# A two-layer HGRN2 and FNet kernel: gates of heads 4 to 15 as two-by-two block products of seven parts

## The chip, the cores and the metric

The kernel runs on one core of a Trainium2 chip. The metric is the time of one execution in device microseconds (us). The engines are named as in the profile: PE (TensorE, matmuls), PEld (its weight loads), DVE (VectorE), ACT (ScalarE), POOL (GpSimd) and SP (SyncE, which issues the DMAs).

## What is computed

There are 512 latent tokens, 256 context tokens, a width of 1024 and two layers. Layer 0 is a bidirectional gated recurrence (HGRN2) of 16 heads of 128, layer 1 a Fourier mixing. The core of the reference for layer 0:

```python
def hgrn_project(h, w_in, lb):
    p = (h @ w_in).reshape(B, N, 5, 16, 128)          # 5 streams, 16 heads
    q = silu(p[0])
    f = lbh + (1.0 - lbh) * sigmoid(p[1:3])           # forget gates, both directions
    return q, 1.0 - f, log(f), p[3], p[4]             # q, k, g, v, z

def hgrn_mixer(h_ctx, h_lat, ...):
    qc, kc, gc, vc, zc = hgrn_project(h_ctx, w_in, lb)
    ql, kl, gl, vl, zl = hgrn_project(h_lat, w_in, lb)
    o_cf, s_cf = chunk_scan(qc, kc[0], vc, gc[0], s0) # context, forward
    o_cb, s_cb = chunk_scan(flip(qc), flip(kc[1]), flip(vc), flip(gc[1]), s0)
    o_lf, _ = chunk_scan(ql, kl[0], vl, gl[0], s_cf)  # latents start from its state
    o_lb, _ = chunk_scan(flip(ql), flip(kl[1]), flip(vl), flip(gl[1]), s_cb)
    y = rms_norm(o_lf + flip(o_lb), norm_g) * silu(zl)
    return heads_joined(y) @ w_out                    # w_out: 2048 x 1024
```

Here h is the RMS-normalized, modulated input of a layer; its output, times a gate row, is added to the residual. Layer 1 is a product, a two-dimensional Fourier transform over tokens and channel groups, and an output product.

## The kernel before

Every matrix product is made in three parts (`mm3`, L94): each fp32 operand is split into a rounded high half and a rest, and hi·hi, hi·lo and lo·hi are added up in PSUM. The tokens after modulation stand transposed in SBUF as `hlh` and `hll` (latents, 8 tiles of 128 x 512) and `hc` (context, 128 x 256), high and low. `Weights` (L59) loads raw weights `wr` of 128 x 1024 into three buffers by SP, and splits them into `wh` (ACT, L56) and `wl` (DVE, L57), one tile ahead of its use.

`projections` takes the heads in pairs: `proj` (L449) of an even head, the pair's values (`proj_v`, tiles `vps`), `proj` of the odd head. A head's projection is two gates, each a latent product `pf` (24 matmuls of 512 columns) and a context product `pfc` (24 of 256), then q and z (`pq`, 24 of 512 each). Head 0 is made in the start.

`scan` (L494) is one head's recurrence, a generator that is stepped once for each projection step (`advance`, L717), so that a head's scan runs beside the next projection: an even head's levels beside the values, an odd head's beside the next head's gates. A scan has seven levels. In a level PE makes `gp` (L578) of `kk` and `z`, DVE multiplies `z` by the decay (L586, two instructions) and takes `gp` into `am` under a mask (L605), and ACT copies the new `kk` (L545), from which the next `gp` comes. Then follow `ktp`, `sp`, `op`, the norm `rstd_o` on POOL (L179, L180), the transposes `otp` and the output `y`.

`ada_rest` (L377) adds up the other modulation rows, `acc` (L401, DVE), from 32 pieces `ar` that are fetched into two buffers. The 13 outputs of the first heads are taken into the output product `o0a` (`out0_early`, `out0_late`) from pairs of `y` in SBUF.

From the end of the start on, a list scheduler sets each engine's order, by dependencies and a priority from the order of the program. An engine carries out its instructions in that order, and waits at one whose inputs are not there.

Of the kernel before, what the change touches and what calls it, by code (L numbers as in the profile page):

```python
# [32 lines left out]
def hgrn_fourier_kernel(ctx: ExitStack, tc: tile.TileContext, a):  # L33
# [25 lines left out]
    class Weights:  # L59
# [5 lines left out]
        def loaded(self, n):  # L65
            while len(self.raw) <= min(n, len(self.specs) - 1):
                src, shape, _ = self.specs[len(self.raw)]
                j = len(self.raw)
                raw = pw.tile(shape, F32, tag="wr", name=f"wr{j}")
                nc.sync.dma_start(out=raw, in_=src)  # L70
                self.raw.append(raw)

        def halves(self, n):
            while len(self.parts) <= min(n, len(self.specs) - 1):
                j = len(self.parts)
                self.loaded(j)
# [48 lines left out]
    masks = pc.tile([P, 7, P], U8, name="masks")  # L125
# [4 lines left out]
    ones_r = pc.tile([P, P], F32R, name="ones_r")  # L130
# [53 lines left out]
    hlh = ph.tile([P, KT, T], F32R, tag="hlh", name="hlh")  # L184
    hll = ph.tile([P, KT, T], F32R, tag="hll", name="hll")
    hc4 = [[ph.tile([P, KT // 2, TC], F32R, tag=f"hc{b}{j}", name=f"hc{b}{j}") for j in range(2)] for b in range(2)]
    hlat = ([hlh[:, k, :] for k in range(KT)], [hll[:, k, :] for k in range(KT)])
    hctx = tuple([hc4[b][k // 4][:, k % 4, :] for k in range(KT)] for b in range(2))
# [45 lines left out]
    def modulate(d, e):  # L234
# [14 lines left out]
    at = {}  # L249

# [44 lines left out]
    with tc.manual_schedule(engines={mybir.EngineType.PE, mybir.EngineType.Activation, mybir.EngineType.DVE}):  # L295
        first = {}

        def product(j, k):
# [3 lines left out]
            mm3(first[st], W.parts[j][0][:, k, :], W.parts[j][1][:, k, :], hlh[:, k, :], hll[:, k, :], k == 0, k == KT - 1)  # L302
# [53 lines left out]
    mraw = p0.tile([P, 7, P], F32, tag="junk", name="mraw")  # L356
    nc.sync.dma_start(out=mraw, in_=a["masks"])
    g.tensor_copy(masks, mraw)
    for t, src in ((own_m, ident), (near_m, mraw[:, 0, :])):
        msum = p0.tile([P, 32], F32, tag="msum", name=f"msum{t.name}", bufs=2) if t is near_m else own_m  # L360
        g.tensor_tensor(out=msum, in0=src[:, 0:32], in1=src[:, 32:64], op=ALU.add)
# [13 lines left out]
    sp = st_hgrn.enter_context(tc.tile_pool(name="sp", bufs=1))  # L375

    def ada_rest():  # L377
# [11 lines left out]
        for j in (0, 1, 2, 3):  # L389
# [4 lines left out]
            for k in range(KT):  # L394
                fetch()
                yield
                raw = raws[j * KT + k]
                if k == 0 and j in (1, 2):
                    v.tensor_scalar(out=acc, in0=raw, scalar1=scol[:, 0, k:k + 1], scalar2=None, op0=ALU.mult)
                else:  # L400
                    v.scalar_tensor_tensor(out=acc, in0=raw, scalar=scol[:, 0, k:k + 1], in1=acc,  # L401
                                           op0=ALU.mult, op1=ALU.add)
            yield
            if j in (0, 3):
                for h in range(2):
                    q = psM(f"gtp{j}_{h}")
                    pe.matmul(q, ones[:, :P], acc[:, h * 512:(h + 1) * 512], start=True, stop=True)
                    s.activation(gates[0 if j == 0 else 1][:, h * 512:(h + 1) * 512], q, AF.Copy)
# [40 lines left out]
    def proj(i):  # L449
        fl = sp.tile([P, 2, T], F32, tag="fl", name=f"fl{i}", bufs=2)  # L450
        z4 = sp.tile([P, 4, T], F32, tag="z4", name=f"z4_{i}", bufs=2)
        fc = sp.tile([P, 2, TC], F32, tag="fc", name=f"fc{i}", bufs=2)

        def gate(src, dst, col):
            s.activation(dst, src, AF.Sigmoid)
            s.activation(dst, dst, AF.Identity, scale=omlb[:, col:col + 1], bias=lbc[:, col:col + 1])

        def ctx_gate(st, wh, wl):
            pcx = (psG if i == 0 else psP)(f"pfc{i}_{st}")
            for k in range(KT):  # L460
# [10 lines left out]
        def silu(pl, dst):  # L471
            s.activation(dst, pl, AF.Sigmoid)
            v.tensor_tensor(out=dst, in0=pl, in1=dst, op=ALU.mult)
            if dst is q:
                v.tensor_tensor(out=z4[:, 0:2, :], in0=fl, in1=q.unsqueeze(1).broadcast_to([P, 2, T]), op=ALU.mult)

        if i == 0:
            for st in (1, 2):
                lat_gate(st, first[st])
            silu(first[0], q)  # L480
            for st in (1, 2):
                wh, wl = W.get(at["w", i, st])
                ctx_gate(st, wh, wl)
            silu(first[3], zs)
            W.get(at["w", i, 3])
            yield scan(i, fl, z4, fc, q, zs)
            return
        for st in (1, 2):
            wh, wl = W.get(at["w", i, st])
            pl = psP(f"pf{i}_{st}")  # L490
            yield from lat_proj(pl, wh, wl, hlh, hll)
            lat_gate(st, pl)
            yield None
            ctx_gate(st, wh, wl)  # L494
            yield None
        for st, dst in ((0, q), (3, zs)):
            wh, wl = W.get(at["w", i, st])
            pl = psP(f"pq{i}_{st}")
            yield from lat_proj(pl, wh, wl, hlh, hll)
# [3 lines left out]
            else:  # L503
                yield scan(i, fl, z4, fc, q, zs)

    def scan(i, fl, z4, fc, q, zs):
        vc = (i % 2) * P
        st = sp.tile([P, 2, NT, P], F32, tag="st", name=f"st{i}")
        kc = fc
        kct = sp.tile([P, 4, P], F32, tag="os", name=f"kct{i}")  # L510

        def ctx_decay():
            v.tensor_tensor_scan(out=rr[:, 0, TC - 2::-1], data0=fc[:, 0, TC - 1:0:-1], data1=ones[:, :TC - 1],
                                 initial=1.0, op0=ALU.mult, op1=ALU.mult)
            v.tensor_tensor_scan(out=rr[:, 1, 1:TC], data0=fc[:, 1, 0:TC - 1], data1=ones[:, :TC - 1],
                                 initial=1.0, op0=ALU.mult, op1=ALU.mult)
            s.activation(kc, fc, AF.Identity, scale=-1.0, bias=1.0)
            v.tensor_tensor(out=kc, in0=kc, in1=rr, op=ALU.mult)

        def ctx_turn():  # L520
            tp = psM(f"ctp{i}")
            for e in range(2):
                for n in range(NTC):
                    b = e * 2 + n
                    pe.transpose(tp[:, b * P:(b + 1) * P], kc[:, e, n * P:(n + 1) * P], ident)
# [43 lines left out]
        tt = fl  # L569
        h = 1  # L570
        for lev in range(7):
            nb = T // h
            gp = None
# [6 lines left out]
            for e in range(2):  # L580
                za = view(z4, e * (T + h), [[2 * T, 2], [2 * h, T // (2 * h)], [1, h]])
                if e == 0:
                    ta = view(tt, 1, [[nb, 2], [2, nb // 2], [0, h]])
                else:
                    ta = view(tt, nb, [[-nb, 2], [2, nb // 2], [0, h]])
                v.tensor_tensor(out=za, in0=za, in1=ta, op=ALU.mult)  # L586
# [20 lines left out]
            v.tensor_tensor(out=tn, in0=view(tt, 0, [[nb, 2], [2, nb // 2]]), in1=view(tt, 1, [[nb, 2], [2, nb // 2]]),  # L607
# [423 lines left out]
```

## Time and profile before

| what | value |
|---|---|
| median of 3 runs | 1209.05 us (1208.63 to 1210.82) |
| the profiled execution | 1208.84 us, span 1207.0 us, mean granted PE clock 0.995 |
| PE busy | 98% of the span |
| DVE busy | 63% |
| ACT busy | 47% |
| POOL busy | 4% |
| read from HBM, written | 115.20 MB, 2.10 MB |

An engine's share is its busy time by the span. Matmuls overlap, so the time from one start to the next tells more than one's duration. Views used below: busy time by stretches of the span, groups of instructions by line and shape (busy us, mean ns | idle time ahead of them and what ended it), single instructions in order of time (start, us), and the waits of an engine.

### The profile page before, as it was taken

The numbers are of one execution on the slowest core, as the hardware profiler recorded it, in microseconds if no ns is written. First come the engines' busy times: TensorE is split into PE (matmuls) and PEld (weight loads), VectorE is DVE, ScalarE is ACT, GpSimd is POOL, SyncE is SP. The second block draws the span as 40 slices with busy tenths as digits, with TensorE's granted clock in tenths as the row PEclk, the third lists the DMA queues.
The fourth block names the chain that finished last, engine by engine and source line by source line (L and its number), as shares of the span: only waits on it lengthen the run. The fifth ranks groups of instructions, "written<-read, shape, count | busy, mean of one in ns | idle before, by whom it ended". The sixth has DMA issues, their size and how long they took to land.

```text
span 1207.0 us, 18983 instructions
## 1 busy us (share of the span) xinstructions
PE 1186.8 (98%) x7677; PEld 1050.8 (87%) x7677; DVE 763.6 (63%) x1250; ACT 562.6 (47%) x1130; POOL 42.8 (4%) x76
## 2 busy tenths in 40 slices
PE   8999999999999999999999999999999999999997
PEld 5699899899889989989988988998888998988885
DVE  5596654665765675686457547458576856668554
ACT  4455544554454453445445455355556533333322
POOL 2100000000000000000000000000000000000000
PEclk9999999999999999999999999999999999999999
DMA  9434211122511521242121112113555314333221
GB/s 358 183 123 141 71 53 53 53 71 70 168 59 31 174 78 53 71 140 71 36 70 53 35 54 70 37 53 107 163 179 182 111 43 134 108 108 120 88 87 70
DMA packets 33673, 118.52 MB, mean 98 GB/s; under 512 B 3879, under 2 KB 4144, under 8 KB 33586
## 3 DMA queue, kind: packets, MB, share of 16 engines
q1 hardware_dynamic: 33586, 117.32, 29.6%
q8 instruction: 60, 0.98, 0.3%
q14 instruction: 27, 0.22, 0.1%
HBM read 115.20 MB, written 2.10 MB: 97 GB/s over the span
## 4 chain that ended last, share of the span: by engine, by line
PE 90%; DVE 4%; DMA 2%; ACT 2%; issue 1%; POOL 1%; SPq 0%; DVEq 0%; POOLq 0%; ACTq 0%
PE gp L578 7%; PE pf L95 4%; PE pq L95 4%; PE pq L97 4%; PE pq L96 4%; PE pf L97 4%; PE pf L96 4%; PE vps L95 4%; PE vps L96 4%; PE vps L97 4%; PE pfc L95 2%; PE pfc L96 2%; PE pfc L97 2%; PE o0a L97 2%; PE o0a L95 2%; PE o0a L96 2%
## 5 line engine op out<-in xcount | busy, mean ns | idle before, releaser
L56 ACT ACTIVATE wh<-wr 128x1024 fp32r<-128x1024 f32 x140 | 148.0, 1058 | 229.9 <-PE pq L96 89.3
L57 DVE TENSOR_TENSOR wl<-wr,wh 128x1024 fp32r<-128x1024 f32 x140 | 170.7, 1220 | 100.4 <-ACT wh L56 100.2
L586 DVE TENSOR_TENSOR z<-z,tt 128x512 f32<-128x512 f32 x192 | 124.0, 687 | 122.3 <-PE gp L578 110.9
L578 PE MATMUL gp<-z,kk 128*128 128x128 f32 x768 | 103.5, 277 | 0.7 <-ACT kk L545 0.6
L578 PEld LDWEIGHTS gp<-z,kk 128*128 128x128 f32 x768 | 97.6, 191 | 6.7 <-ACT kk L545 3.3
L95 PE MATMUL pf<-hlh,wh 128*128 128x512 f32 x240 | 99.2, 413 | 0.0
L95 PE MATMUL pq<-hlh,wh 128*128 128x512 f32 x240 | 97.1, 405 | 0.0
L545 ACT ACTIVATE kk<-z 128x512 f32<-128x512 f32 x96 | 61.8, 644 | 71.5 <-DVE z L586 71.3
L97 PE MATMUL pf<-hlh,wl 128*128 128x512 f32 x240 | 94.5, 394 | 0.0
L97 PE MATMUL pq<-hlh,wl 128*128 128x512 f32 x240 | 93.9, 391 | 0.0
L96 PE MATMUL pf<-hll,wh 128*128 128x512 f32 x240 | 93.7, 391 | 0.0
L96 PE MATMUL pq<-hll,wh 128*128 128x512 f32 x240 | 93.5, 390 | 0.0
L95 PE MATMUL pfc<-hc,wh 128*128 128x256 f32 x256 | 74.8, 292 | 0.0
L95 PE MATMUL vps<-wh,hlh 128*128 128x256 f32 x256 | 74.2, 291 | 0.0
L97 PE MATMUL vps<-wh,hll 128*128 128x256 f32 x256 | 72.6, 283 | 0.0
L96 PE MATMUL vps<-wl,hlh 128*128 128x256 f32 x256 | 72.5, 283 | 0.0
L96 PE MATMUL pfc<-hc,wh 128*128 128x256 f32 x256 | 72.4, 283 | 0.0
L97 PE MATMUL pfc<-hc,wl 128*128 128x256 f32 x256 | 72.4, 283 | 0.0
L97 PEld LDWEIGHTS pf<-hlh,wl 128*128 128x128 f32 x240 | 45.0, 188 | 10.4 <-issue 0.2
L97 PEld LDWEIGHTS pq<-hlh,wl 128*128 128x128 f32 x240 | 45.1, 188 | 10.0
L95 PEld LDWEIGHTS pf<-hlh,wh 128*128 128x128 f32 x240 | 45.2, 188 | 9.5 <-issue 1.9
L96 PEld LDWEIGHTS pf<-hll,wh 128*128 128x128 f32 x240 | 45.3, 189 | 8.2 <-issue 0.2
(268 smaller groups left out, 2994.0 us busy)
## 6 DMA issues: line engine op xcount, KB each, us to landing
wr<-hg_w SPq DMA_DIRECT2D x64, 512.0 KB, 3.5
ar<-ada_r SPq DMA_DIRECT2D x32, 512.0 KB, 3.8
wr<-ft_w SPq DMA_DIRECT2D x32, 512.0 KB, 4.0
wr<-hg_wout SPq DMA_DIRECT2D x29, 512.0 KB, 3.5
wa<-ada_a SPq DMA_DIRECT2D x16, 512.0 KB, 10.5
wr<-hg_v SPq DMA_DIRECT2D x16, 512.0 KB, 3.4
wr<-ft_wout SPq DMA_DIRECT2D x16, 512.0 KB, 3.5
xs<-x SPq DMA_DIRECT2D x4, 512.0 KB, 3.7
```

What stands on the lines that cost most here:

```text
L56: s.activation(hi, src, AF.Copy)
L57: v.tensor_tensor(out=lo, in0=src, in1=hi.bitcast(F32), op=ALU.subtract)
L95: pe.matmul(out, lh, rh, start=first, stop=False)
L96: pe.matmul(out, lh, rl, start=False, stop=False)
L97: pe.matmul(out, ll, rh, start=False, stop=last)
L545: s.activation(view(kk, 0, [[2 * h, T // (2 * h)], [h, 2], [1, h]]), view(z4, 2 * T, [[2 * h, T // (2 * h)], [T + h, 2], [1, h]]), AF.Copy)
L578: pe.matmul(gp[:, n * P:(n + 1) * P], kk[:, n * P:(n + 1) * P], view(z4, n * P, dims), start=True, stop=True)
L586: v.tensor_tensor(out=za, in0=za, in1=ta, op=ALU.mult)
```

## The change

For heads 4 to 15 the two gate weights (as 2 x 2 blocks of four k-tiles each) times the tokens (2 x 2 blocks: k-tiles 0 to 3 and 4 to 7, by even and odd tiles of 128 tokens, latents and context joined to 768 columns) are made with seven products, `px`, in place of eight. Each has 12 matmuls of 384 columns (three runs of 128), so a head has 84 of them for 48 of 512 and 48 of 256.

- `blocks` makes the products and puts them together: two copies on ACT, five adds on DVE and two on POOL, each of 128 x 384; the sums stand in `ff` (768 columns a direction), and sigmoid and lower bound run over all 768.
- `fold_piece` makes the mixed weight pieces in place in the raw tiles (four DVE instructions of 128 x 512 a head). There are seven pieces of 128 x 512 to split for two weights of 128 x 1024, taken up to four ahead.
- `mixes`, stepped every second projection step, makes four mixed token blocks once, in four rounds over the first heads: POOL adds high and low (2 x 128 x 768, into `whole`, in the buffers that `ar` and `acc` use later) and mixes (4 x 128 x 384); then four splits on ACT and DVE.
- `ar` has one buffer, its fetch follows the accumulation before, `ada_rest` begins after step 40, and two of its first products move to ACT.
- `y` of heads 0 to 12 is written to DRAM (`yd`) and fetched back in pieces of 128 x 256; the gate rows go through DRAM (`grow`).
- `ks` and `pn` take `kk`'s buffers; `am`'s copies of level 0 come ahead of the first `kk`; the masks are loaded and cast earlier, five of seven planes.

```diff
+                if j in pieces:
+                    both = pw.tile([P, 2, KT // 2, P], F32R, tag="wh" if pieces[j] % 2 else "wl", name=f"wp{j}")
+                    hi, lo = both[:, 0], both[:, 1]
...
-            self.halves(n + 1)
+            if n in pieces and pieces[n] < 5:
+                self.halves(min(n + 4, n + 6 - pieces[n]))
+            else:
+                self.halves(n + 2 if n + 2 in pieces else n + 1)
...
+    def fold_piece(w, j):
+        p = pieces[j]
+        w.loaded(j - p + 1)
+        f1, f2 = w.raw[j - p], w.raw[j - p + 1]
+        a11, a12, a21, a22 = f1[:, :4], f1[:, 4:], f2[:, :4], f2[:, 4:]
+        if p == 2:
+            v.tensor_tensor(out=a21, in0=a21, in1=a22, op=ALU.add)
+            v.tensor_tensor(out=a11, in0=a21, in1=a11, op=ALU.subtract)
+        elif p == 4:
+            v.tensor_tensor(out=a21, in0=a22, in1=a11, op=ALU.subtract)
+        elif p == 5:
+            v.tensor_tensor(out=a12, in0=a12, in1=a11, op=ALU.subtract)
+        return (a11, a12, a11, a21, a21, a12, a22)[p]
+
+    def head_specs(i):
+        if i < PLAIN:
+            for st in (1, 2):
+                spec(("w", i, st), a["hg_w"][i, st], [P, KT, P])
+        else:
+            for p in range(7):
+                pieces[len(specs)] = p
+                spec(("f", i, p), a["hg_w"][i, 1 + p] if p < 2 else None, [P, KT, P], fold_piece)
...
+    grow = [pd.tile([1, D], F32, name=f"grow{j}") for j in range(2)]
+    gates = [None, None]
+    yd = [pd.tile([P, T], F32, name=f"yd{i}") for i in range(13)]
...
+    def mixes():
+        for t in range(4):
+            mix[t] = [ph.tile([P, KT // 2, N // 2], F32R, tag=f"t{2 * t + b}", name=f"mix{t}_{b}") for b in range(2)]
+        for k in range(KT // 2):
+            whole = []
+            for e, tag in enumerate(("ar", "acc")):
+                t = sp.tile([P, D], F32, tag=tag, name=f"whole{k}_{e}")
+                kk = 4 * e + k
+                g.tensor_tensor(out=t[:, :N], in0=hlh[:, kk, :].bitcast(F32), in1=hll[:, kk, :].bitcast(F32), op=ALU.add)
+                w = t[:, :N].rearrange("p (n e c) -> p e n c", e=2, c=P)
+                whole += [w[:, 0], w[:, 1]]
+            b11, b12, b21, b22 = whole
+            yield
+            g.tensor_tensor(out=b22, in0=b22, in1=b12, op=ALU.subtract)
+            g.tensor_tensor(out=b12, in0=b12, in1=b11, op=ALU.subtract)
+            g.tensor_tensor(out=b11, in0=b22, in1=b11, op=ALU.add)
+            g.tensor_tensor(out=b21, in0=b21, in1=b11, op=ALU.subtract)
+            yield
+            for t, src in ((2, b22), (0, b12), (1, b11), (3, b21)):
+                split(*(mix[t][b][:, k, :].rearrange("p (n c) -> p n c", c=P) for b in range(2)), src)
+                if t in (0, 3):
+                    yield
...
-                raw = sp.tile([P, D], F32, tag="ar", name=f"ar{j}_{k}", bufs=2)
+                raw = sp.tile([P, D], F32, tag="ar", name=f"ar{j}_{k}")
...
-                fetch()
...
-                    v.tensor_scalar(out=acc, in0=raw, scalar1=scol[:, 0, k:k + 1], scalar2=None, op0=ALU.mult)
+                    s.activation(acc, raw, AF.Copy, scale=scol[:, 0, k:k + 1])
                 else:
                     v.scalar_tensor_tensor(out=acc, in0=raw, scalar=scol[:, 0, k:k + 1], in1=acc,
                                            op0=ALU.mult, op1=ALU.add)
+                fetch()
...
+    def blocks(i, ff, gate):
+        base = at["f", i, 0]
+        nh = N // 2
+
+        def out(st, half):
+            return ff[:, 2 - st].rearrange("p (n e c) -> p e n c", e=2, c=P)[:, half]
+
+        def tri(t):
+            return t[:, :nh].rearrange("p (n c) -> p n c", c=P)
+
+        def prod(p, rhs):
+            acc = psP(f"px{i}_{p}")
+            hi, lo = W.get(base + p)
+            for k in range(KT // 2):
+                mm3(tri(acc), hi[:, k, :], lo[:, k, :], rhs(0, k), rhs(1, k), k == 0, k == KT // 2 - 1)
+            return acc
+
+        def block(kh, half):
+            return lambda b, k: tiled[b][:, kh * 4 + k, half]
+
+        def mixed(t):
+            return lambda b, k: mix[t][b][:, k, :].rearrange("p (n c) -> p n c", c=P)
+
+        def kept(acc, name):
+            c = sp.tile([P, nh], F32, tag="cc", name=f"{name}{i}", bufs=2)
+            s.activation(c, acc[:, :nh], AF.Copy)
+            return c
+
+        def add(eng, dst, x, y):
+            eng.tensor_tensor(out=dst, in0=x, in1=y, op=ALU.add)
+
+        u = kept(prod(0, block(0, 0)), "u")
+        yield None
+        add(v, out(1, 0), tri(prod(1, block(1, 0))), tri(u))
+        yield None
+        add(v, u, prod(2, mixed(1))[:, :nh], u)
+        yield None
+        c5 = kept(prod(3, mixed(0)), "c5")
+        add(g, out(1, 1), tri(u), tri(c5))
+        yield None
+        add(v, u, prod(4, mixed(2))[:, :nh], u)
+        add(g, out(2, 1), tri(u), tri(c5))
+        yield None
+        add(v, out(1, 1), tri(prod(5, block(1, 1))), out(1, 1))
+        s.activation(ff[:, 1, :], ff[:, 1, :], AF.Sigmoid)
+        gate(1)
+        yield None
+        add(v, out(2, 0), tri(prod(6, mixed(3))), tri(u))
+        s.activation(ff[:, 0, :], ff[:, 0, :], AF.Sigmoid)
+        gate(2)
+        yield None
...
-        if i % 2 == 0:
-            ypair[0] = py.tile([P, 2, T], F32, tag=f"yp{i // 2}", name=f"y{i}")
-        y = ypair[0][:, i % 2, :]
+        y = py.tile([P, T], F32, tag="y" if i < LAST else f"y{i}", name=f"y{i}")
+        if i < LAST:
+            nc.sync.dma_start(out=yd[i], in_=y)
...
+    def y_fetch(k, r, ahead):
+        n = back[r].index((k, r))
+        for kk, _ in back[r][:n + 1 + ahead]:
+            if (kk, r) not in got:
+                t = got[kk, r] = (fp if r else sp).tile([P, 256], F32, tag="yr" if r else "cc", name=f"yr{r}_{kk}",
+                                                        bufs=3 if r else 2)
+                nc.sync.dma_start(out=t, in_=yd[kk][:, r * 256:(r + 1) * 256])
+        return got[k, r]
...
-        if step > 30 and step % 3 == 0:
+        if step % 2 == 0:
+            next(mix_work, None)
+        if step > 40 and step % 3 == 0:
             next(side_work, None)
```

Where instructions move. First DVE during head 3's levels, which run beside head 4's gates (z_3 and am are head 3's, px and u head 4's; a name's last number is an instance). Before:

```order
L605 COPY_PREDICATED am_2211<-masks,gp_1_2254 128x512 [waits Activation_49]
L586 TENSOR_TENSOR z_3_1891<-z_3_1891,tt_1_2264 128x2x64x4 [waits PE_49,Activation_49]
L586 TENSOR_TENSOR z_3_1891<-z_3_1891,tt_1_2264 128x2x64x4 [waits DVE_49]
L605 COPY_PREDICATED am_2211<-masks,gp_2_2300 128x512 [waits DVE_49]
L57 TENSOR_TENSOR wl_2422<-wr_2194,wh_2421 128x1024 [waits DMAHW4_49,Activation_49]
L513 SCALAR_TENSOR_TENSOR rr<-fc_2187,ones 128x255 [waits Activation_49]
L586 TENSOR_TENSOR z_3_1891<-z_3_1891,tt_2_2310 128x2x32x8 [waits PE_49,Activation_49]
```

Now:

```order
L725 COPY_PREDICATED am_2270<-masks,gp_1_2316 128x512 [waits Activation_49]
L603 TENSOR_TENSOR u_2266<-px_2_2335,u_2266 128x384 [waits DVE_49,PE_49]
L59 TENSOR_TENSOR wl_2466<-wr_2399,wh_2465 128x1024 [waits DMAHW4_49,Activation_49]
L706 TENSOR_TENSOR z_3_1949<-z_3_1949,tt_1_2326 128x2x64x4 [waits PE_49,Activation_49]
L706 TENSOR_TENSOR z_3_1949<-z_3_1949,tt_1_2326 128x2x64x4 [waits DVE_49]
L725 COPY_PREDICATED am_2270<-masks,gp_2_2352 128x512 [waits DVE_49]
L706 TENSOR_TENSOR z_3_1949<-z_3_1949,tt_2_2362 128x2x32x8 [waits PE_49,Activation_49]
L706 TENSOR_TENSOR z_3_1949<-z_3_1949,tt_2_2362 128x2x32x8 [waits DVE_49]
L725 COPY_PREDICATED am_2270<-masks,gp_3_2380 128x512 [waits DVE_49]
L603 TENSOR_TENSOR u_2266<-px_4_2398,u_2266 128x384 [waits PE_49,Pool_49]
L59 TENSOR_TENSOR wl_2506<-wr_2431,wh_2505 128x1024 [waits DMAHW6_49,Activation_49]
L706 TENSOR_TENSOR z_3_1949<-z_3_1949,tt_3_2390 128x2x16x16 [waits PE_49,Activation_49]
```

The adds of `px_2` and `px_4` and a whole split each have come between one level's z and the next; the second of the adds also waits for POOL.

Then DVE during head 5's levels, with `acc` of `ada_rest` (now; before, these levels hold no `acc`):

```order
L725 COPY_PREDICATED am_3243<-masks,gp_1_3292 128x512 [waits Activation_49]
L466 SCALAR_TENSOR_TENSOR acc_3179<-ar_2_3372,scol,acc_3179 128x1024 [waits DMAHW5_49,DVE_49]
L603 TENSOR_TENSOR u_3239<-px_2_3308,u_3239 128x384 [waits DVE_49,PE_49]
L706 TENSOR_TENSOR z_5_2911<-z_5_2911,tt_1_3302 128x2x64x4 [waits PE_49,Activation_49]
L706 TENSOR_TENSOR z_5_2911<-z_5_2911,tt_1_3302 128x2x64x4 [waits DVE_49]
L725 COPY_PREDICATED am_3243<-masks,gp_2_3325 128x512 [waits DVE_49]
L59 TENSOR_TENSOR wl_3439<-wr_3375,wh_3438 128x1024 [waits DMAHW0_49]
L466 SCALAR_TENSOR_TENSOR acc_3179<-ar_3_3479,scol,acc_3179 128x1024 [waits DMAHW7_49,DVE_49]
```

Each `acc` waits for a fetch that starts after the `acc` before it, and the next level's z stands behind it.

Last, ACT during head 0's levels 3 and 4 (`kk_16` makes gp_4, `kk_32` gp_5). Before:

```order
L545 ACTIVATE kk_16_900<-z_0_643 128x512 [waits DVE_49,Activation_49]
L56 ACTIVATE wh_993<-wr_727 128x1024 [waits DMAHW1_49,PE_49]
L545 ACTIVATE kk_32_943<-z_0_643 128x512 [waits DVE_49,Activation_49]
L440 ACTIVATE vt_722<-vps_4_911 128x512 [waits PE_49]
L56 ACTIVATE wh_1098<-wr_733 128x1024 [waits DMAHW5_49]
```

Now:

```order
L664 ACTIVATE kk_16_912<-z_0_642 128x512 [waits DVE_49,Activation_49]
L58 ACTIVATE mix_0_790<-whole_1_1118 128x384 [waits Pool_49]
L58 ACTIVATE mix_0_786<-whole_0_1116 128x384 [waits Pool_49]
L58 ACTIVATE mix_0_788<-whole_0_1116 128x384 [waits Pool_49]
L58 ACTIVATE mix_0_792<-whole_1_1118 128x384 [waits Pool_49]
L664 ACTIVATE kk_32_955<-z_0_642 128x512 [waits DVE_49,PE_49,Activation_49]
```

Four copies of the mixing's second round, each of which waits for POOL, have come ahead of `kk_32`. On POOL, head 0's `rstd_o` now stands behind all 24 adds of the mixing; before, nothing stood ahead of it but the start's work.

More of the change, by code (lines that the diff above doesn't have):

```diff
@@ L181, in rstd_of @@
         return r
[L184 to L188, printed above, removed]
+    N = T + TC
+    hlh = ph.tile([P, KT, N], F32R, name="hlh")
+    hll = ph.tile([P, KT, N], F32R, name="hll")
+    tiled = [t.rearrange("p k (n e c) -> p k e n c", e=2, c=P) for t in (hlh, hll)]
+    mix = [None] * 4
+    hlat = ([hlh[:, k, :T] for k in range(KT)], [hll[:, k, :T] for k in range(KT)])
+    hctx = ([hlh[:, k, T:] for k in range(KT)], [hll[:, k, T:] for k in range(KT)])
     acol = pc.tile([P, KT, 2], F32, name="acol")
@@ L315, in hgrn_fourier_kernel @@
             nc.sync.dma_start(out=xs[:, NT + n, :], in_=a["ctx"][n * P:(n + 1) * P, :])
+        mraw = p0.tile([P, 5, P], F32, name="mraw")
+        nc.sync.dma_start(out=mraw, in_=a["masks"][:, :5, :])
         keep_warm(24, "warm1")
@@ L348, in hgrn_fourier_kernel @@
             product(j, KT - 1)
+        g.tensor_copy(masks, mraw[:, 1:])
+        for t, src in ((own_m, ident), (near_m, mraw[:, 0, :])):
+            msum = p0.tile([P, 32], F32, tag="msum", name=f"msum{t.name}", bufs=2) if t is near_m else own_m
+            g.tensor_tensor(out=msum, in0=src[:, 0:32], in1=src[:, 32:64], op=ALU.add)
+            for j in (64, 96):
+                g.tensor_tensor(out=msum, in0=msum, in1=src[:, j:j + 32], op=ALU.add)
+            if t is near_m:
+                g.tensor_copy(near_m, msum)
         for d in range(2):
@@ L407, in ada_rest @@
                     pe.matmul(q, ones[:, :P], acc[:, h * 512:(h + 1) * 512], start=True, stop=True)
-                    s.activation(gates[0 if j == 0 else 1][:, h * 512:(h + 1) * 512], q, AF.Copy)
+                    s.activation(acc[0:1, h * 512:(h + 1) * 512], q[0:1, :], AF.Copy)
+                nc.sync.dma_start(out=grow[0 if j == 0 else 1], in_=acc[0:1, :])
             else:
@@ L498, in proj @@
             pl = psP(f"pq{i}_{st}")
-            yield from lat_proj(pl, wh, wl, hlh, hll)
+            yield from lat_proj(pl, wh, wl, hlh[:, :, :T], hll[:, :, :T])
             silu(pl, dst)
@@ L666, in acc_of, with y_parts @@
         return acc0[m, hf]
-    def y_parts(k, r):
-        y2 = pw.tile([P, 2, 256], F32R, tag="yh", name=f"o0y{r}_{k}", bufs=2)
-        split(y2[:, 0], y2[:, 1], ys[k][:, r * 256:(r + 1) * 256])
+    back = [(k, 0) for k in range(LAST)], [(k, 1) for k in range(LAST)]
+    got = {}
+    def y_fetch(k, r, ahead):
[6 more added lines that the diff above has]
+        return got[k, r]
+    def y_parts(k, r, late=True):
+        y2 = (fp if late else sp).tile([P, 2, 256], F32R, tag="o0y" if late else "q", name=f"o0y{r}_{k}", bufs=2)
+        src = ys[k][:, r * 256:(r + 1) * 256] if k >= LAST else y_fetch(k, r, 2 if late else 1)
+        split(y2[:, 0], y2[:, 1], src)
         return y2
@@ L759, in hgrn_fourier_kernel @@
         nc.sync.dma_start(out=x1[:, n, :], in_=a["x"][n * P:(n + 1) * P, :])
+    for j in range(2):
+        gates[j] = fp.tile([P, D], F32, tag=f"gate{j}", name=f"gate{j}")
+        nc.sync.dma_start(out=gates[j], in_=grow[j].broadcast_to([P, D]))
     def residual(n, acc):
```

161 lines of the change are left out of this document (83 added, 78 removed).

## The prediction

> **What bounds the kernel now.** I read the page's first section, then busy time by stretch, then the waits of TensorE, then groups and single rows.
>
> ```profile
> PE 1186.8 (98%) x7677; PEld 1050.8 (87%) x7677; DVE 763.6 (63%) x1250; ACT 562.6 (47%) x1130; POOL 42.8 (4%) x76
> ```
>
> Busy time by stretch (from:to, then its length, PE, PEld, DVE, ACT, POOL, granted clock, DMA share, GB/s): 65 to 120 is head 0's scan beside the first values and head 1; 120 to 860 the other heads.
>
> ```profile
> 65.00:120.00 55.00, 55.00 (x416) 51.26 (x416) 41.45 (x65) 31.56 (x67) 1.22 (x2) 1.00 0.45 144
> 120.00:300.00 180.00, 180.00 (x1236) 162.46 (x1235) 110.42 (x183) 88.69 (x189) 3.61 (x6) 1.00 0.20 61
> 300.00:600.00 300.00, 298.92 (x2062) 270.71 (x2062) 197.63 (x314) 144.49 (x316) 9.00 (x12) 1.00 0.28 89
> 600.00:860.00 260.00, 260.00 (x1731) 232.99 (x1730) 155.81 (x261) 131.23 (x282) 7.80 (x12) 1.00 0.21 65
> ```
>
> TensorE idles 1.1 of the 795 us from 65 to 860, so time taken out of its queue there is time off the kernel, until something else is late. The next engine, VectorE, has 464 of 740 us from 120 to 860 (63%). The list of what TensorE waits for has one entry in the level chain:
>
> ```profile
> PE gp L578 <- ACT kk L545: 0.6, 1, 0.6
> ```
>
> **The change, part by part.**
>
> *Gates of heads 4 to 15 on TensorE.* Single matmuls of one gate, 512 columns (latent) and 256 (context), start to start:
>
> ```profile
> 400.11 0.28 PE L95 MATMUL pfc<-hc,wh 128*128 128x256 f32 x1
> ...
> 402.51 0.28 PE L97 MATMUL pfc<-hc,wl 128*128 128x256 f32 x1
> 407.62 0.40 PE L96 MATMUL pf<-hll,wh 128*128 128x512 f32 x1
> ...
> 409.90 0.39 PE L97 MATMUL pf<-hlh,wl 128*128 128x512 f32 x1
> ```
>
> The first pair is 20 steps in 2.40 us, 0.120 us a matmul; the second 10 steps in 2.28, 0.228. For 384 columns, which no row shows, I take the middle, 0.174 (bounds 0.120 and 0.228). A head's two gates are now 48 matmuls of each: 48 x 0.228 + 48 x 0.120 = 16.7 us. Seven products of 12 are 84 x 0.174 = 14.6. That is 2.1 us a head, **-25.1 us** for twelve.
>
> *What VectorE pays.*
>
> ```profile
> L57 DVE TENSOR_TENSOR wl<-wr,wh 128x1024 fp32r<-128x1024 f32 x140 | 170.7, 1220 | 100.4 <-ACT wh L56 100.2
> L57 DVE TENSOR_TENSOR o1y<-yf,o1y 128x512 fp32r<-128x512 f32 x16 | 10.9, 681 | 0.0
> L57 DVE TENSOR_TENSOR o0y<-y,o0y 128x256 fp32r<-128x256 f32 x32 | 13.5, 421 | 8.3 <-ACT o0y L56 8.2
> L586 DVE TENSOR_TENSOR z<-z,tt 128x512 f32<-128x512 f32 x192 | 124.0, 687 | 122.3 <-PE gp L578 110.9 <-ACT wh L56 10.9 <-PE ctp L525 0.2
> L623 ACT ACTIVATE kt<-ktp 128x384 f32<-128x384 f32 x32 | 14.7, 487 | 0.0
> ```
>
> Two splits at 1.22 become seven at 0.68, with four folds at 0.68 and five adds of 384 columns, between 0.42 and 0.68, say 0.55: 10.3 for 2.4, so 7.8 a head, 94 in all. 464 becomes 558 of some 715 us, 78%. ScalarE gets two copies at 0.49 and seven short copies for two long ones, some 2 us a head over its 364 of 740. Both lie beside TensorE's work on the average; the question is the level chain. Here it is for head 5 (start, length):
>
> ```profile
> 333.45 1.12 PE L578 MATMUL gp<-z,kk 128*128 128x128 f32 x8
> 334.68 1.29 DVE L586 TENSOR_TENSOR z<-z,tt 128x512 f32<-128x512 f32 x2 [3.36 <-PE gp L578]
> 335.89 0.74 DVE L605 COPY_PREDICATED am<-masks,gp 128x512 f32<-128x512 uint8 x1
> 336.01 0.63 ACT L545 ACTIVATE kk<-z 128x512 f32<-128x512 f32 x1 [0.25 <-DVE z L586]
> 337.29 0.94 PE L578 MATMUL gp<-z,kk 128*128 128x128 f32 x7
> ```
>
> From gp to z 1.2 us, z 1.3, kk 0.7, and 0.1 to the next gp: about 3.2 us. Today two gp starts lie 3.84 us apart, because half a projection stands between them; that is the cover. An odd head's levels will run between the next head's products, and there TensorE has only 12 x 0.174 + 1.0 (gp) = 3.1 us. So the chain is late by 0.1 us a level, and by more where VectorE has other rows ahead of z: the two wl of the order above each put 0.74 + 0.55 + 1.22 + 1.29 = 3.8 us between one z's end and the next's, 0.7 over. Summed over the five gaps shown by the order, some of them shorter, I take 1 us for each of the six odd heads 3 to 13: **+6 us** (0 to 12).
>
> *The single `ar` buffer.* Now a fetch starts only when the accumulation before it is over.
>
> ```profile
> ar<-ada_r SPq DMA_DIRECT2D x32, 512.0 KB, 3.8
> L401 DVE SCALAR_TENSOR_TENSOR acc<-ar,scol,acc 128x1024 f32<-128x1024 f32 x30 | 38.4, 1280 | 10.0 <-DMA ar<-ada_r 9.9
> ```
>
> Behind a waiting acc stand the next z pair and with it gp. A level's rows on VectorE (1.3 + 0.7 + 0.6 + 0.7) cover 3.3 of the 3.8 us and of the issue ahead of them; where the order puts an acc into every level (heads 1 and 5), it waits about 0.5 us, six times: **+3** (0 to 8).
>
> *The mixtures, heads 0 to 3.* POOL gets 8 adds of 768 columns and 16 of 384. The trace has no such add; its nearest rows:
>
> ```profile
> L358 POOL CAST masks<-mraw 128x896 uint8<-128x896 f32 x1 | 1.5, 1470 | 0.6 <-DMA mraw<-masks 0.6
> L881 POOL MEMSET wmh<- 128x1024 f32 x1 | 1.0, 954 | 0.0
> L361 POOL TENSOR_TENSOR own_m<-ident 128x32 f32<-128x32 f32 x1 | 0.2, 250 | 1.6 <-DMA ident<-ident 1.6
> ```
>
> No input costs 0.93 ns an element, one input 1.64; a second one by the same step gives 2.35, so 1.8 and 0.9 us. The low end is one input's 1.26 and 0.63. A round is 2 x 1.8 + 4 x 0.9 = 7.2 us (low 5.0). The Trainium skill (GPSIMD Engine Reference, 3.1) gives 4497 ns for an add of 2048 fp32; by that 384 columns would be about 0.84 us and the round 6.8, an estimate from that page alone.
>
> In the order ScalarE's copies of round 1 (counted from 0) stand ahead of kk_32, and so of gp_5. Today head 0's gp_5 starts here:
>
> ```profile
> 93.53 1.09 PE L578 MATMUL gp<-z,kk 128*128 128x128 f32 x8
> ```
>
> Round 1 can't begin before VectorE has split round 0 (behind gp_3's z, about 87 to 89.5). Two adds at 1.8, four at 0.9 bring its last part to about 95, the last copy and kk_32 to 96, and gp_5 to 96.2: 2.7 us late. Round 2 in front of kk_64 makes gp_6 late by 2.1 in the same way. Low: 1.2 and 0.4. High: 12 in all, if VectorE and POOL hold each other up. I take **+6**. TensorE's cover is the value products, which run on only until gp stands first in its queue.
>
> Whether they do hold each other up:
>
> ```profile
> 468.58 0.19 POOL L179 TENSOR_SCALAR rstd_o<-oss 128x4 f32<-128x4 f32 x1 [52.67 <-ACT os L644]
> 514.28 1.10 POOL L179 TENSOR_SCALAR rstd_o<-oss 128x4 f32<-128x4 f32 x1 [44.42 <-ACT os L644]
> 514.04 1.28 DVE L401 SCALAR_TENSOR_TENSOR acc<-ar,scol,acc 128x1024 f32<-128x1024 f32 x1
> ```
>
> An operation of 0.19 us took 1.10, from 514.28 to 515.38, while VectorE's acc ran from 514.04 to 515.32: POOL got through when VectorE had ended. What a long POOL add does to VectorE no row of two inputs shows. The Trainium skill (SBUF — State Buffer, Who interferes with whom) says that a VectorE instruction with two SBUF inputs and a GpSimd one that reads SBUF exclude each other for the whole instruction. That speaks against this change, and the two rows agree with it on POOL's side.
>
> *Outputs through DRAM, gate rows, start.* 13 writes and 26 fetches of a piece lie beside TensorE work, one to two ahead; a late one costs one landing, 3.5 us by the weights' rows. The start loses the masks' cast from its end and has the same TensorE rows. Together **+2** (-1 to 5).
>
> **Sum.** -25.1 + 6 + 3 + 6 + 2 = -8.1. The profiled execution took 1208.84 us (0.2 under the median 1209.05), which gives 1200.7: **1201 us**. Its own range from the bounds, not all ends at once: 1192 to 1209.
>
> **Rivals.** (B) *The cover holds*: z, acc and POOL's rounds hide nearly always, as the one wait of 0.6 us in today's list suggests. Then -25.1 + 4, or 1188. Against it: 3.1 us of TensorE beside a chain of 3.2.
> (C) *Slower: POOL and VectorE exclude each other.* The place is the z pair of every level. 24 mixing adds (8 x 1.8 + 16 x 0.9 = 29 us) and two gate adds at 0.9 for twelve heads (22 us) are 51 us in which VectorE's two-input rows stand still. The gate adds run in the tightest steps. If all the 51 us came on top of the terms above, the time would be 1252; from a share of 8.1 / 51 = 16% on the gain is gone, and at a quarter, 13 us, the time is 1214. For it: the row of 1.10 us. Against: VectorE is idle 22% even then, and the mixing's share is partly in my +6.
> (D) *VectorE becomes the bound of the block steps*: in each of the twelve heads TensorE waits about 0.7 us more for px's adds, folds and pieces, or 8 us: 1209, no change.
> (E) *The change doesn't do what it says*: a moving operand of three separate runs of 128 columns goes no faster than 512. 84 x 0.228 = 19.2, 2.5 more than now, so +30 + 17, or 1256. No row of such an operand is there to exclude it.
>
> **How the numbers follow.** Forecast 0.46, B 0.15, C 0.21, D 0.14, E 0.04. The range leaves out E, C's far part and B's lowest: 1185 to 1218. About 0.2%, 2.4 us, is what a measurement of this kernel can tell from no change. Faster: B and most of the forecast, 0.60; same: D and the forecast's upper end, 0.16; slower: C, E and a tail of D, 0.24.
>
> **What would show it.** px starts 0.174 us apart, or 0.228 for E. TensorE's waits: gp on kk and z, 12 us or so in all; gp_5 and gp_6 of head 0 late behind POOL's whole. POOL's adds at 1.8 and 0.9, and VectorE's z longer than 0.69 beside them for C. VectorE's acc waiting on ar 0.5 us in heads 1 and 5. The 65 to 120 stretch no longer full for TensorE. The prediction is wrong if a 384-column matmul isn't near 0.174, if z keeps its 0.69 and TensorE stays full (B), or if it idles over 25 us (C, D).

## The result and the profile after

The changed kernel took 1225.74 us (median of 4 runs, 1223.84 to 1227.40) beside 1209.32 for the kernel before: a ratio of 1.0139, 95% interval 1.0126 to 1.0151. It is 16 us slower; the forecast was 8 us faster, and the time lies above the range. The profiled execution took 1225.33 us, its span 1223.5.

The page's first section, busy us and share of the span:

```profile
PE 1180.2 (96%) x7533; PEld 1052.3 (86%) x7533; DVE 867.2 (71%) x1432; ACT 589.9 (48%) x1176; POOL 113.5 (9%) x124
```

TensorE has 144 instructions and 6.6 us less than before (1186.8), VectorE 104 us more, POOL 71 more. Busy time by stretch, columns as in the prediction:

```profile
65.00:120.00 55.00, 43.30 (x317) 40.40 (x316) 44.78 (x54) 27.71 (x54) 33.69 (x22) 0.94 0.13 39
120.00:300.00 180.00, 176.28 (x1190) 158.24 (x1189) 126.49 (x210) 87.25 (x192) 10.92 (x13) 1.00 0.26 83
300.00:600.00 300.00, 294.50 (x2005) 272.15 (x2004) 240.83 (x400) 158.95 (x338) 26.34 (x24) 1.00 0.31 99
600.00:860.00 260.00, 258.21 (x1720) 237.20 (x1719) 190.80 (x331) 143.19 (x303) 20.68 (x20) 1.00 0.26 84
```

In the stretch from 65 to 120, where the mixing lies, TensorE was full and now idles 11.7 us. In the list of its waits the level chain has moved to the top:

```profile
PE gp L698 <- ACT kk L664: 16.3, 21, 4.8
PE ktp L742 <- ACT st L655: 2.5, 5, 0.6
```

Where the time went is seen best at a point that every head passes once, the column sums `cs` of its level 0. The first fence is the kernel before, the second the changed one; in each the upper row is head 1's and the lower head 15's:

```profile
131.39 0.43 PE L553 MATMUL cs<-ks,ones 128*32 128x128 f32 x8
...
824.57 0.43 PE L553 MATMUL cs<-ks,ones 128*32 128x128 f32 x8
```

```profile
149.46 0.43 PE L672 MATMUL cs<-ks,ones 128*32 128x128 f32 x8
...
837.29 0.43 PE L672 MATMUL cs<-ks,ones 128*32 128x128 f32 x8
```

Head 1 comes 18.1 us late, before the first product of blocks; head 15 12.7 late; the end of the span 16.5. So the start and the mixing lost 18 us, the heads from there to head 15 won back only 5.4, and the tail lost 4 more.

**The mixing.** Four z pairs of VectorE in head 0's levels, which took 1.28 to 1.29 us each before the change:

```profile
85.88 1.29 DVE L706 TENSOR_TENSOR z<-z,tt 128x512 f32<-128x512 f32 x2 [0.15 <-PE gp L698]
...
89.24 2.84 DVE L706 TENSOR_TENSOR z<-z,tt 128x512 f32<-128x512 f32 x2 [0.33 <-PE gp L698]
...
94.12 3.06 DVE L706 TENSOR_TENSOR z<-z,tt 128x512 f32<-128x512 f32 x2 [0.89 <-PE gp L698]
...
104.41 3.74 DVE L706 TENSOR_TENSOR z<-z,tt 128x512 f32<-128x512 f32 x2
```

POOL at the same time:

```profile
89.08 1.84 POOL L428 TENSOR_TENSOR whole<-hlh,hll 128x768 f32<-128x768 f32 x1 [13.27 <-DVE mix L59]
93.37 1.83 POOL L428 TENSOR_TENSOR whole<-hlh,hll 128x768 f32<-128x768 f32 x1 [2.45 <-DVE mix L59]
95.28 1.34 POOL L433 TENSOR_TENSOR whole<-whole,whole 128x384 f32<-128x384 f32 x1
...
103.43 2.76 POOL L428 TENSOR_TENSOR whole<-hlh,hll 128x768 f32<-128x768 f32 x1 [0.50 <-DVE mix L59]
```

The pair from 85.88 ran alone. The next one, from 89.24, is longer by 1.55 us, and POOL's add that runs to 90.92 lies over its first 1.68 us. The pair from 94.12 is longer by 1.77; one add lies over its start, the next (95.28 to 96.62) wholly within it. The trace of single instructions shows the pattern: of the 192 z in all heads 14 take over 0.8 us, before the change none, and every one of the 14 ends 0.55 us behind the end of a POOL add. ScalarE's copies of the mixing, in the order ahead of kk, then add their own wait, and so does TensorE:

```profile
100.60 0.52 ACT L58 ACTIVATE mix<-whole 128x384 fp32r<-128x384 f32 x1 [0.74 <-POOL whole L436]
101.03 0.61 ACT L664 ACTIVATE kk<-z 128x512 f32<-128x512 f32 x1
```

```profile
101.69 2.07 PE L698 MATMUL gp<-z,kk 128*128 128x128 f32 x8 [4.81 <-ACT kk L664]
112.06 2.08 PE L698 MATMUL gp<-z,kk 128*128 128x128 f32 x8 [4.05 <-ACT kk L664]
```

gp_5 started at 93.53 before; it is now 8.2 late, and gp_6, at 97.53 before, 14.5. Both also take twice their 1.1 us: right behind the idle times of 4.8 and 4.1 the granted clock is 0.50, in the windows from 101.7 to 103.8 and from 112.0 to 114.2.

**The block heads.** Here are head 5's levels on VectorE, then POOL:

```profile
354.18 1.28 DVE L466 SCALAR_TENSOR_TENSOR acc<-ar,scol,acc 128x1024 f32<-128x1024 f32 x1 [0.94 <-DMA ar<-ada_r]
355.38 0.55 DVE L603 TENSOR_TENSOR u<-px,u 128x384 f32<-128x384 f32 x1
355.84 1.28 DVE L706 TENSOR_TENSOR z<-z,tt 128x512 f32<-128x512 f32 x2
...
364.17 2.11 DVE L706 TENSOR_TENSOR z<-z,tt 128x512 f32<-128x512 f32 x2
```

```profile
358.33 1.42 POOL L603 TENSOR_TENSOR ff<-u,c 128x384 f32<-128x384 f32 x1 [27.66 <-ACT c L599]
363.19 1.94 POOL L603 TENSOR_TENSOR ff<-u,c 128x384 f32<-128x384 f32 x1 [3.45 <-DVE u L603]
```

The acc waits 0.94 us for its single buffer and then runs ahead of z; the z pair from 364.17 is 0.83 us longer beside a POOL add, which itself took 1.94.

### The profile page after: what moved, and what is told of

It reads as the page before. It is cut to its first block, busy times and chain, and to the rows that moved or that the text cites. A ratio compares the mean times of both kernels' runs of the same rounds, so it can differ in the third digit from the quotient of the medians.

```text
span 1223.5 us, 19181 instructions
## 1 busy us (share of the span) xinstructions
PE 1180.2 (96%) x7533; PEld 1052.3 (86%) x7533; DVE 867.2 (71%) x1432; ACT 589.9 (48%) x1176; POOL 113.5 (9%) x124
## 4 chain that ended last, share of the span: by engine, by line
PE 72%; DVE 13%; ACT 7%; issue 3%; DMA 3%; POOL 2%; SPq 0%; DVEq 0%; POOLq 0%; ACTq 0%
PE gp L698 5%; DVE z L706 4%; PE pq L108 3%; PE vps L106 3%; PE pq L107 3%; PE pq L106 3%; PE vps L108 3%; PE vps L107 3%; PE px L106 3%; PE px L107 3%; PE px L108 3%; PE o0a L108 2%; PE o0a L106 2%; PE o0a L107 2%; PE o1a L107 2%
## 5 line engine op out<-in xcount | busy, mean ns | idle before, releaser
L698 PE MATMUL gp<-z,kk 128*128 128x128 f32 x768 | 108.5, 285 | 16.6 <-ACT kk L664 16.3
L106 PE MATMUL vps<-wh,hlh 128*128 128x256 f32 x384 | 111.8, 292 | 0.0
L107 PE MATMUL vps<-wl,hlh 128*128 128x256 f32 x384 | 108.8, 283 | 0.0
L108 PE MATMUL vps<-wh,hll 128*128 128x256 f32 x384 | 108.7, 283 | 0.0
L58 ACT ACTIVATE wp<-wr 128x512 fp32r<-128x512 f32 x84 | 52.0, 627 | 66.4 <-PE pq L107 64.2
L106 PEld LDWEIGHTS vps<-wh,hlh 128*128 128x128 f32 x384 | 73.4, 191 | 1.4 <-issue 1.4
L59 DVE TENSOR_TENSOR wp<-wr,wp 128x512 fp32r<-128x512 f32 x84 | 56.3, 686 | 25.3 <-ACT wp L58 24.9
L107 PEld LDWEIGHTS vps<-wl,hlh 128*128 128x128 f32 x384 | 73.5, 191 | 0.3
L108 PEld LDWEIGHTS vps<-wh,hll 128*128 128x128 f32 x384 | 73.4, 191 | 0.2 <-issue 0.2
L603 POOL TENSOR_TENSOR ff<-u,c 128x384 f32<-128x384 f32 x24 | 36.4, 1518 | 383.0 <-ACT c L599 365.8
L106 PE MATMUL px<-mix,wp 128*128 128x384 f32 x192 | 67.9, 354 | 0.0
L107 PE MATMUL px<-mix,wp 128*128 128x384 f32 x192 | 65.8, 343 | 0.0
L108 PE MATMUL px<-mix,wp 128*128 128x384 f32 x192 | 64.9, 338 | 0.0
```

The lines of the kernel that those rows point to most:

```text
L58: s.activation(hi, src, AF.Copy)
L59: v.tensor_tensor(out=lo, in0=src, in1=hi.bitcast(F32), op=ALU.subtract)
L106: pe.matmul(out, lh, rh, start=first, stop=False)
L107: pe.matmul(out, lh, rl, start=False, stop=False)
L108: pe.matmul(out, ll, rh, start=False, stop=last)
L603: eng.tensor_tensor(out=dst, in0=x, in1=y, op=ALU.add)
```

## The experiments

Two theories were tested. **L**: POOL and VectorE shut each other out, wherever both read SBUF. **Q**: the order is to blame, that is, ScalarE's copies ahead of kk and VectorE's new rows ahead of z, whoever makes the adds. All ratios are to the kernel before, which ran beside each.

### e1: the mixing's adds on VectorE

```diff
-                g.tensor_tensor(out=t[:, :N], in0=hlh[:, kk, :].bitcast(F32), ...)
+                v.tensor_tensor(out=t[:, :N], in0=hlh[:, kk, :].bitcast(F32), ...)
...
-            g.tensor_tensor(out=b22, in0=b22, in1=b12, op=ALU.subtract)
+            v.tensor_tensor(out=b22, in0=b22, in1=b12, op=ALU.subtract)
```

(and the three after it in the same way)

> The 24 adds of the mixing stand on VectorE in place of POOL, nothing else. Theory L (POOL and VectorE shut each other out): the z pairs of head 0 go back to 1.28 us, the adds take 0.5 to 1.0 us each and not 1.0 to 2.0, and of the 13 us that head 0's scan lost at least half comes back: about 1217. Theory Q (it is the order: ScalarE's copies of the mixing wait ahead of kk whoever makes the adds): VectorE has 16 us more, heads 0 to 1 stay 13 us behind, 1225 or above.

1208.82 us, ratio 0.9996 (0.9986 to 1.0006): the whole loss is gone, and head 0's z pairs are back at 1.28 to 1.29 us. TensorE's stretch from 65 to 120 is nearly full again:

```profile
65.00:120.00 55.00, 54.43 (x414) 50.83 (x413) 50.94 (x91) 35.32 (x76) 1.39 (x2) 1.00 0.15 49
```

By ratio it gains 1.4% on the changed kernel, some 17 us, more than L asked. The order of ScalarE changed with it, though (the copies of the second round stand behind kk_32 here), so e1 alone doesn't part the theories. e7 does.

### e2: the gate adds on VectorE

```diff
-        add(g, out(1, 1), tri(u), tri(c5))
+        add(v, out(1, 1), tri(u), tri(c5))
...
-        add(g, out(2, 1), tri(u), tri(c5))
+        add(v, out(2, 1), tri(u), tri(c5))
```

> The two adds of each block head that POOL made are made by VectorE, nothing else. Theory L: each add held the z pair beside it some 0.8 us (2.11 for 1.28 us in one level of head 5) and itself took 1.5; without them twelve heads get back up to 1.6 us each, less 1.1 us of new VectorE work: 1213 to 1222. Theory Q: VectorE's rows between two z are the cost, two more of 0.55 us make it worse: 1226 to 1235.

1220.77 us, 1.0094 (1.0078 to 1.0109). With 13 us more work on VectorE the kernel is 5 us faster (0.45% of 1209): as L has it, at the small end.

### e3 and e4: plain gates, with and without the mixing

e3 makes every head's gates plainly; the mixtures are made, and nothing reads them. e4 leaves them out too:

```diff
-    PLAIN = 4
+    PLAIN = 16
```

```diff
-            next(mix_work, None)
+            pass
```

> All heads' gates are made plainly (48 matmuls of 512 and 48 of 256 columns); the mixtures are still made, and nothing reads them. With the next run it gives the mixing by itself: 13 us by where head 1 starts in the changed kernel, so 1226 to 1230. Against the changed kernel it gives what the blocks are worth: 25 us by the matmuls alone, 6 by the heads' starts.

> Plain gates everywhere and no mixtures: what is left of the change is the outputs and gate rows through DRAM, the single ar buffer, the gates joined to 768 columns and the shared kk buffers. By head 0's start (5 us late) and the tail (4 us) this costs up to 9: 1214 to 1218. If POOL's mixing already made the start late, only the tail's 4 and some of ar stay: 1211 to 1214.

e3 1233.48 us, 1.0201 (1.0184 to 1.0218); e4 1214.34, 1.0044 (1.0029 to 1.0059). This takes the change apart:

| part | from | us |
|---|---|---|
| DRAM path, single ar, joined gates, shared buffers | e4 to before | +5.4 |
| the mixing on POOL | e3 to e4 | +19.1 |
| blocks in place of plain gates | after to e3 | -7.7 |

The mixing was 6 us dearer than I read from where head 1 starts. Nothing reads its result in e3, so its price is what making it does to head 0, beside which it runs: 17.4 us of it are there by head 1's cs (149.26 in e3, 131.86 in e4). In e4 head 0's cs is 3.2 us late (77.20 for 74.01) and head 15's 1.0, so most of the start's loss is made up by then; the rest, 4.2 us, comes behind head 15's cs, about half in the output product and half in layer 1.

### e5: both on VectorE, POOL left with the norms

The edits of e1 and e2 together.

> The mixing's 24 adds and the block heads' 24 adds all stand on VectorE; POOL keeps only the norms. Theory L (exclusion of POOL and VectorE): both gains add up, 1208.8 less some 5, so 1202 to 1206, and no z pair in heads 4 to 15 is longer than 1.3 us but for those beside a norm. Theory Q (order and VectorE's own rows): VectorE has 13 us more than in e1, no gain on e1: 1208 or above.

1205.37 us, 0.9966 (0.9955 to 0.9978): faster than before by 4 us, and by 3.6 than e1, with 13 us more on VectorE. The z group over all heads, in the changed kernel and in e5:

```profile
L706 DVE TENSOR_TENSOR z<-z,tt 128x512 f32<-128x512 f32 x192 | 135.6, 747 | 63.2 <-PE gp L698 60.3 <-ACT wh L58 1.2 <-ACT ff L554 0.8
```

```profile
L706 DVE TENSOR_TENSOR z<-z,tt 128x512 f32<-128x512 f32 x192 | 123.9, 686 | 57.8 <-PE gp L698 57.0 <-ACT wh L58 0.7
```

747 ns has become 686, the 687 of before. As L expects.

### e6: two buffers for ar

```diff
-                t = sp.tile([P, D], F32, tag=tag, name=f"whole{k}_{e}")
+                t = sp.tile([P, D], F32, tag=tag, name=f"whole{k}_{e}", bufs=2 - e)
...
-                raw = sp.tile([P, D], F32, tag="ar", name=f"ar{j}_{k}")
+                raw = sp.tile([P, D], F32, tag="ar", name=f"ar{j}_{k}", bufs=2)
...
             for k in range(KT):
+                fetch()
                 yield
...
-                fetch()
...
-        y = py.tile([P, T], F32, tag="y" if i < LAST else f"y{i}", name=f"y{i}")
+        y = sp.tile([P, T], F32, tag="os", name=f"y{i}") if i < LAST else py.tile([P, T], F32, tag=f"y{i}", name=f"y{i}")
```

> As e5, with two buffers for ar, each fetched one step ahead as before the change (y of heads 0 to 12 takes the buffer of os, which makes room). If the waits for ar in the level chains of heads 1 to 11 cost what head 5 shows (z late by 1.4 and 1.7 us in two levels), five pairs of heads get 2 to 3 us each: 1192 to 1198. If an acc ahead of z costs its 1.28 us whether its data are there or not, or the chains hide it, less than 3 us: 1200 to 1206.

1202.77 us, 0.9940 (0.9926 to 0.9955), 2.6 us under e5: the smaller of the two gains expected. VectorE's idle time ahead of acc, in e5 and in e6:

```profile
L466 DVE SCALAR_TENSOR_TENSOR acc<-ar,scol,acc 128x1024 f32<-128x1024 f32 x30 | 38.4, 1278 | 6.1 <-DMA ar<-ada_r 6.1
```

```profile
L467 DVE SCALAR_TENSOR_TENSOR acc<-ar,scol,acc 128x1024 f32<-128x1024 f32 x30 | 38.3, 1278 | 1.0 <-DMA ar<-ada_r 0.9
```

Five of VectorE's six waiting us are gone; the gain in time is half of that.

### e7: adds on POOL that nothing reads

```diff
+                d = sp.tile([P, N], F32, tag="shadow", name=f"shadow{k}_{e}")
+                g.tensor_tensor(out=d, in0=hlh[:, kk, :].bitcast(F32), in1=hll[:, kk, :].bitcast(F32), op=ALU.add)
+                for j in range(2):
+                    g.tensor_tensor(out=d[:, :N // 2], in0=hlh[:, kk, :N // 2].bitcast(F32),
+                                    in1=hll[:, kk, :N // 2].bitcast(F32), op=ALU.add)
```

(e7 and e9 are e5 with these lines and, as in e6, `y` in the buffer of `os`; the time of e9 shows that this buffer alone changes nothing.)

> As e5 (with y in os's buffer), and POOL makes 24 adds of the mixing's shapes from hlh and hll into a buffer that nothing reads, one behind the other from 66 us on. No instruction waits for them but head 0's norm behind them, so what e7 is over e5 is exclusion alone, without ScalarE's copies ahead of kk. Theory L: 24 adds take 36 us on POOL, VectorE's z pairs there grow from 1.29 to about 3, gp starts lie 5 us apart and not 3.3; 10 to 17 us over e5. Theory Q: what cost 13 us was the order on ScalarE; under 4 us over e5.

1227.37 us, 1.0145 (1.0128 to 1.0162), 22 us over e5, though only a norm waits for the result of POOL: more than L expected. The z pairs of head 0's first levels:

```profile
96.97 2.89 DVE L711 TENSOR_TENSOR z<-z,tt 128x512 f32<-128x512 f32 x2
102.75 3.55 DVE L711 TENSOR_TENSOR z<-z,tt 128x512 f32<-128x512 f32 x2
108.37 1.29 DVE L711 TENSOR_TENSOR z<-z,tt 128x512 f32<-128x512 f32 x2
```

POOL's adds end at 107.2; the first pair behind them is back at 1.29. So POOL's adds alone, with no copy of ScalarE waiting for them, can cost as much as the whole loss. They don't cost it at the same place, though: they begin at 64.8 and run on without a pause, so that half of the loss comes before head 0's level 0, whose cs starts at 87.87 for 77.53 in e5. There VectorE's split of a weight is held, and TensorE with it:

```profile
75.79 4.76 DVE L59 TENSOR_TENSOR wl<-wr,wh 128x1024 fp32r<-128x1024 f32 x2
78.67 0.58 PE L107 MATMUL vps<-wl,hlh 128*128 128x256 f32 x1 [6.38 <-DVE wl L59]
```

In the changed kernel head 0's cs starts at 79.02, and most of the loss lies behind it. Also, e7's idle times bring the granted clock to 0.81 from 65 to 120, where it is 1.00 in e5: the 22 us hold what the clock adds.

### e9: as long on POOL, without inputs

```diff
-                g.tensor_tensor(out=d, ...)
-                for j in range(2):
-                    g.tensor_tensor(out=d[:, :N // 2], ...)
+                for j in range(7):
+                    g.memset(d, float(j))
```

> As e7, but POOL makes 56 memsets of 768 columns (0.7 us each, 40 us in all) in place of its 24 adds: as long on POOL, with no input. If only POOL's reads shut VectorE's two-input instructions out, z stays at 1.29 us and the time at e5's, 1204 to 1207. If any POOL instruction does, or POOL's length is what head 0's norm behind it costs, as e7: 1220 or above.

1205.21 us, 0.9959 (0.9942 to 0.9975): the time of e5. POOL is as busy as in e7 (groups: e7's shadow adds together 40.5 us), and z is untouched:

```profile
L709 DVE TENSOR_TENSOR z<-z,tt 128x512 f32<-128x512 f32 x192 | 124.0, 687 | 57.9 <-PE gp L701 56.9 <-ACT wh L58 0.7
...
L431 POOL MEMSET shadow<- 128x768 f32 x56 | 41.5, 741 | 16.3 <-DVE hll L261 13.2
```

So POOL's being busy costs nothing, nor does the norm behind it; an add that reads SBUF does. The Trainium skill (SBUF — State Buffer, Who interferes with whom) says just this: a VectorE instruction with two SBUF inputs contends with a GpSimd instruction that reads SBUF, and not with one that only writes. e7 and e9 agree.

### e10: the mixing on VectorE, plain gates

e1 with

```diff
-    PLAIN = 4
+    PLAIN = 16
```

> Plain gates everywhere, the mixtures made on VectorE and not read: beside e4 the price of mixing there. By where head 1 starts in e1 (1.0 us behind e4) it is 0 to 2: 1214 to 1216.5. If the exclusion was not the cause of the mixing's 19 us, 1220 or above.

1216.69 us, 1.0058 (1.0041 to 1.0074). Beside e4's 1.0044 the mixing on VectorE costs 1.7 us, which the two intervals don't tell from nothing. On POOL it cost 19.

### e8: e6 with the state's copies on VectorE

```diff
-            s.activation(st[:, 0, 0, :], sps[:, :P], AF.Copy)
-            s.activation(st[:, 1, NT - 1, :], sps[:, P:2 * P], AF.Copy)
+            v.tensor_copy(st[:, 0, 0, :], sps[:, :P])
+            v.tensor_copy(st[:, 1, NT - 1, :], sps[:, P:2 * P])
```

> e6 with the two copies of the context state (st, 128 x 128 each) on VectorE and not on ScalarE, where they stand behind the gates of 768 columns. In e6 ktp waits for them: TensorE's steps ahead of ktp are 0.85 us too long in a pair of heads. If that wait is real time, six pairs give back 3 to 5 us: 1198 to 1200. If the next instruction is late anyway, or VectorE's rows push z: 1202 to 1204.

1201.41 us, 0.9929 (0.9912 to 0.9946), between the two cases and not told from e6. In the pair of heads around 450 us the wait of ktp has gone; instead the transposes of the norm's result wait longer, 0.91 us for 0.35:

```profile
467.58 1.10 PE L772 MATMUL otp<-ident,os 128*128 128x128 f32 x4 [0.91 <-ACT os L768]
```

A wait has moved to the next chain. Still, e6 and e8 beat both kernels: 0.6 and 0.7% under the kernel before.

## Why the prediction was wrong, point by point

- **Gates on TensorE, -25.1: right.** The first of these px starts at 310.68, the last 10 starts later, so 0.174 us each; rival E falls. In e6, in the 390 us from head 5's cs to head 13's, TensorE's time from start to start adds up to 123.3 us for px, and to 140.0 for pf and pfc before: -16.6 for eight heads, 2.1 each as forecast. This is the time of the products alone; what the kernel got of it stands below.

```profile
310.68 0.34 PE L107 MATMUL px<-hll,wp 128*128 128x384 f32 x1
...
312.42 0.33 PE L108 MATMUL px<-hlh,wp 128*128 128x384 f32 x1
```

- **The mixtures, +6: the step that failed.** "I take +6" became +19.1. The adds' own lengths were near: 1.8 us alone for 768 columns, and 1.0 for 384 (the last round). What was left out is that VectorE's two-input rows, the z pairs first, stood still for as long as such an add ran, and that they held the adds in turn: 1.0 became up to 1.96. So gp_5 came 8.2 us late, where the sum had 2.7, and gp_6 another 6.3, where it had 2.1. The high end of 12 named this and was still too low. With the adds on VectorE the same mixing costs 1.7 or nothing (e10); e7 shows that POOL's adds can do it without ScalarE's copies behind them. How much of the 19 ScalarE's order and the lower clock behind long idle times make was not parted.
- **The blocks, -25.1 and +6, missed by nearly as much**: -7.7 in the changed kernel (e3), for the -19 of the two terms, so 11 of the 25 us between forecast and result against the 13 of the mixtures. With nothing on POOL but the norms they are worth 11 (e10 to e5). The rest of the 25.1 went to POOL's gate adds (rival C), the single ar and the chains named below.
- **Rival C, 0.21, was the mechanism, at the right place** (z), and the row of 1.10 us that I had shown for it was its sign. I gave it too little, because VectorE has idle time on the average. But the z pairs lie in a chain of 3.2 us that has no idle time. Its price of 1214 at "a quarter" of 51 us was low; mixing and gate adds on POOL cost some 17 (e1) and 4 to 5 (e2, e5 to e1).
- **Level chain, +6, and the single ar, +3: near in size, but not the only loss.** In the changed kernel gp waits for kk 6.3 us outside head 0 (16.3 less 10.0), with POOL's gate adds and ar in it. ar costs 2.6 (e6 to e5). In e6, without POOL's adds and the wait for ar, eight heads still gain 9.5 us in all and not 16.6. The other 7 appear, by the times from start to start, mostly ahead of ktp (2.7), otp (2.5) and gp (2.0). I take it that TensorE's steps have become too short there for the chains of ScalarE and the norm that ran under them; the prediction had no term for ktp and otp. That is about rival D's price, not D's place: VectorE is busy 72% and does not end these waits. Rival B, that the cover holds everywhere, falls with it. What each of these chains costs is not settled; e8 took one away and the next was late.
- **Outputs through DRAM and start, +2: +5.4 by e4** with the joined gates and ar in it, 4.2 of it in the tail. That +2 and ar's +3 come near it is luck: no term stood for the tail. Its cause there was not followed further.

The sum by the runs: 5.4 + 19.1 - 7.7 = 16.8, and measured 16.4.

## What to carry to other kernels

Before work is moved to an engine that is idle, look for what it shares with the engine of the critical chain: here POOL at 4% was the wrong place for an add of two inputs in SBUF, and VectorE at 63% nearly free. One instruction that takes over five times its length beside another engine's, as the norm's 1.10 for 0.19 us, is worth a test of its own before it is priced. And when the bound engine's steps get shorter, every chain that ran under them has to be measured against the new step.

## What the runs showed of the hardware

- Adds of POOL and two-input instructions of VectorE, with their inputs in SBUF, hold each other up: z pairs of 1.29 us take up to 3.7, each of the 14 long z ends 0.55 us behind a POOL add, and POOL's adds of 1.0 us take up to 1.96. Memsets of POOL, 41.5 us of them, change nothing.
- A matmul whose moving operand is three runs of 128 columns starts every 0.174 us, halfway between 256 and 512 columns in one run.
- Right behind idle times of 4.8 and 4.1 us the granted clock is 0.50 over the next 2 us, and eight matmuls take 2.07 us for 1.1.
